# Two projection sums in the double PSUM bank, and a mean square scaled in two steps

## The chip, the core and the metric

The kernel runs on one core of a Trainium2 chip. The metric is the device time of one execution in microseconds (us). TensorE (PE, with its weight loads as PEld) multiplies matrices, VectorE (DVE), ScalarE (ACT) and GpSimd (POOL) do the rest, and SyncE (SP) issues most of the transfers. PSUM, which takes the results of TensorE, has eight banks of 128 x 512 fp32 numbers here.

## The reference

A decoder trunk of two layers on a sequence of 1024 rows with 1024 channels, batch 1, fp32:

```python
for layer in range(2):
    u = rmsnorm(h, norm_w[layer])
    h = h + (ssd_diffattn_mixer if layer == 0 else hgrn2_mixer)(u, ...)
return rmsnorm(h, final_norm_w)
```

Layer 0 projects `u` to a chunked state-space scan (16 heads of 64) and to a differential attention (8 heads of 128); the two branches' 1024 channels each are concatenated and mapped by one output projection, 2048 to 1024. Layer 1 is a gated linear recurrence with 16 heads of 128; its 2048 channels go through another output projection, 2048 to 1024. `rmsnorm(x, w)` is `x * rsqrt(mean(x*x) + 1e-6) * w`.

## The kernel before

Every product is done to fp32 accuracy out of three: both factors are split into a high and a low part (`w_hi`, `w_lo`, and likewise the data), and hi x hi, hi x lo and lo x hi are summed in one PSUM bank.

**Order of the work.** The program is written in order and then given to a planner. The planner simulates the engines with its own costs and, on each engine, takes the earliest written instruction that is ready and for whose new tile a buffer is free; the engines then run these orders as they are, each strictly in order. So products of the output projection stand in TensorE's queue between those of the last heads, wherever the planner saw TensorE free. Only the scan's stretch of TensorE has an order written by hand.

**PSUM.** `BANKS` gives the eight banks to three names: `pj`, two tiles of one bank; `s1`, two of one bank; `big`, two of two banks. `pj` takes sums of projections (L176 for the input projections, L187 for the output projection). `s1` takes transposes and small products. `big` takes, in layer 0, the scan's second step and the attention's scores: `att_core` asks for two `big` tiles for each of its eight blocks of 128 queries (L613, one for each softmax map), and VectorE frees one by adding the bias and taking maxima (L617, L621). In layer 1 `hgrn_core` uses `big` three times per head (L1054, L1090, L1096, L1142).

**The output projection** (`out_proj`, once per layer) has four quarters: two halves of the 2048 input channels (first half, second half) times two halves of the 1024 output columns (`n`). A quarter is one call of `sums`: eight sums, one for each 128 rows, taken in pairs `t = 0, 2, 4, 6`. A sum is 24 matmuls of 512 columns: two weight tiles (`kq`) times four channel blocks times three products. In the first and the last pair the order is first weight tile for both sums, then second weight tile for both. A finished sum is added by VectorE to the residual `x1`, in layer 0's first half times the scan's `rs_a` (L767), in layer 1's first half as it is (L765), in both second halves at L782. The `x1` tiles are loaded at L763 into buffers that earlier work frees. The first half needs only the scan (layer 0) or heads 0 to 7 (layer 1), so its products can run while the last heads are still computed; the data come in by `load_y` (L706 to L713). The input projections of attention head 7 are the last users of `pj` ahead of it (L579, L580 take them out).

**The norm that follows.** In the second half, ScalarE squares each updated row block and sums it (L784) into `ss[hf][:, t, n]`. When `n = 1` is done, VectorE adds the two halves (L789), scales and adds the epsilon (L149, in `rstd`), and GpSimd raises to the power -1/2 (L150). The result scales the rows: for layer 1's input (L877, L879) or for the output (L1001, L1002, stored at L1004).

Of the kernel before, what the change touches and what calls it, by code (L numbers as in the profile page):

```python
# [15 lines left out]
ALU = mybir.AluOpType  # L16
# [5 lines left out]
D = 1024  # L22
NT = L // P
KT = D // P
EPS = 1e-6
# [673 lines left out]
def load_y(S, y_d, wcols, hf, k, tags):  # L699

    nc = S.nc
    tiles = []
    for j, tag in enumerate(tags):
        y = S.t(tag, [P, 2, 512], F32R)
        raw = y[:, 1].bitcast(F32)
        nc.sync.dma_start(raw, y_d(k + j, 1)[0, :, hf * 512:hf * 512 + 512])  # L706
        if wcols is not None and k < KT:
            w = wcols[:, k + j:k + j + 1]
            nc.scalar.activation(y[:, 0], raw, AF.Identity, scale=w)
            nc.vector.scalar_tensor_tensor(y[:, 1], raw, w, y[:, 0].bitcast(F32), op0=ALU.mult, op1=ALU.subtract)  # L710
        else:
            nc.scalar.copy(y[:, 0], raw)
            nc.vector.tensor_tensor(y[:, 1], raw, y[:, 0].bitcast(F32), op=ALU.subtract)  # L713
        tiles.append(y)
    return tiles


def out_proj(S, y_d, wcols, x_d, x1_tags, rs_a, finish):


    nc = S.nc
    load = lambda hf, k, *tags: load_y(S, y_d, wcols, hf, k, tags)

    def pair():
        i = S.wpos
        S.wpos += 2
        S._wprep(i)
        S._wprep(i + 1)
        return S.wtiles[i], S.wtiles[i + 1]

    def sums(ws, ys):

        for t in range(0, NT, 2):
            pas = [S.ps("pj") for _ in range(2)]
            order = ((0, 0), (1, 0), (0, 1), (1, 1)) if t in (0, NT - 2) else ((0, 0), (0, 1), (1, 0), (1, 1))
            for j, kq in order:
                hf, tt = divmod(t + j, 4)
                y = ys[hf][4 * kq:4 * kq + 4]
                S.mm_tm(pas[j], ws[kq], *([z[:, i, tt * P:tt * P + P] for z in y] for i in range(2)),
                        first=kq == 0, last=kq == 1)  # L740
                if t == NT - 2 and j == 1:
                    S._wprep(S.wpos + kq)
                if kq == 1:
                    yield hf, tt, pas[j]

    y = [[], []]
    for hf in range(2):
        for k in range(0, KT, 2):
            y[hf] += load(hf, k, "u", "u")
        if hf == 0:  # L750
            ws = pair()

    x1s = {}
    tags = iter(x1_tags)
    late = [[], []]
    for n in range(2):
        if n:
            ws = pair()
        for hf, t, pa in sums(ws, y):
            if t % 2 == 0:  # L760
                x1 = x1s[hf, n, t // 2] = S.t(next(tags), [P, 2, 512])
                r0 = hf * 512 + t * P
                nc.sync.dma_start(x1, x_d[r0:r0 + 256, n * 512:n * 512 + 512].rearrange("(t p) n -> p t n", p=P))  # L763
            if rs_a is None:
                nc.vector.tensor_tensor(x1[:, t % 2], pa, x1[:, t % 2], op=ALU.add)  # L765
            else:
                nc.vector.scalar_tensor_tensor(x1[:, t % 2], pa, rs_a[:, hf * 4 + t:hf * 4 + t + 1], x1[:, t % 2],  # L767
                                               op0=ALU.mult, op1=ALU.add)
            if n == 1 and t % 2 == 1:
                k = 4 * hf + t - 1  # L770
                late[0] += load(0, KT + k, *(("A", "A") if k < 6 else ("u", "u")))
    tags1 = "V", "V", "G", "G", "p0", "p0", "p1", "wT"
    ss = [S.sm.tile([P, 4, 2], F32, name="ss4", bufs=2) for _ in range(2)]
    for n in range(2):
        ws = pair()
        rss = []
        for hf, t, pa in sums(ws, late):
            if n == 0 and hf == 0:
                for k in (2 * t, 2 * t + 1):
                    late[1] += load(1, KT + k, tags1[k])  # L780
            xr = x1s[hf, n, t // 2][:, t % 2]
            nc.vector.tensor_tensor(xr, pa, xr, op=ALU.add)  # L782
            jk = S.t("ey", [P, 512])
            nc.scalar.activation(jk, xr, AF.Square, accum_out=ss[hf][:, t, n:n + 1])  # L784
            if n == 0:
                finish.early(xr)
                continue
            sr = S.sm.tile([P, 1], F32, name="sr")
            nc.vector.tensor_tensor(sr, ss[hf][:, t, 0:1], ss[hf][:, t, 1:2], op=ALU.add)  # L789
            rs = S.sm.tile([P, 1], F32, name="rs")  # L790
            S.rstd(rs, sr, 1.0 / D, EPS)
            rss.append(rs)
            finish.row(hf, t, [x1s[hf, m, t // 2][:, t % 2] for m in range(2)], rs)
            if t == 3:
                finish(hf, x1s, rss)
                rss = []
# [93 lines left out]
def layer0(S, x, x1_d, u1):  # L890
# [34 lines left out]
    for h in range(8):  # L925
# [9 lines left out]
        elif h < 7:  # L935
            Vn = S.proj_v(u)
        tail = att_core(S, h, qk, V, sg[h % 2], yb[h], tail)
    tail()
    out_proj(S, lambda k, n: (ya if k < 8 else yb)[k % 8:k % 8 + n], S.ssdw, x,
             ["V", "V", "bt"] + ["A"] * 5, rsa,  # L940
             next_norm(S, u1, x1_d, S.norm_c[:, 8:16]))


def layer1(S, x1_d, u, out):
# [63 lines left out]

    finish.early, finish.row = early, row
    out_proj(S, lambda k, n: yo[k:k + n], None, x1_d, ["V", "V"] + ["A"] * 5 + ["bt"], None, finish)  # L1010


# [185 lines left out]
```

## Time and profile before

| | |
|---|---|
| median of 3 runs | 2192.46 us (2192.11 to 2192.67) |
| the profiled execution: its own time | 2190.09 us |
| its span, first to last instruction | 2188.2 us |
| TensorE busy | 2149.8 us, 98% |
| VectorE, ScalarE, GpSimd busy | 57%, 38%, 10% |
| granted TensorE clock, mean | 0.999 |

The profiled execution took 1.9 us more than its span, and 2.4 us less than the median of the runs. Times in the rows count from the span's start. A row of a timeline names the instruction's start and length, engine, line, operation, what is written `<-` what is read, and shapes; `[0.76 <-DVE w_lo L135]` says that the engine sat idle for 0.76 us before it, until that instruction ended. Lengths of matmuls overlap, since they are pipelined: back to back, one of 512 columns starts about 0.23 us after the other.

### The profile page before, as it was taken

What the parts mean: (1) busy time and instruction counts of PE and PEld (TensorE: products, weight loads), DVE (VectorE), ACT (ScalarE), POOL (GpSimd) and SP (SyncE); (2) the same over time, 40 slices, a digit from 0 to 9 for tenths busy, and PEclk for the clock granted to TensorE, in tenths of its full rate; (3) what the DMA queues carried; (4) which work ended last, traced back from release to release, by engine and by line L of the source; (5) the groups of instructions that cost most, each with busy time, mean ns of one, the idle gap of its engine ahead of it and who ended that gap; (6) DMA issues with size and microseconds to landing.
All of it is one profiled execution on the core that took longest, in us unless ns stands there. A gap on an engine that the chain in (4) does not pass through costs nothing.

```text
span 2188.2 us, 37614 instructions
## 1 busy us (share of the span) xinstructions
PE 2149.8 (98%) x15332; PEld 1827.5 (84%) x15332; DVE 1248.3 (57%) x2816; ACT 826.0 (38%) x1863; POOL 211.9 (10%) x216
## 2 busy tenths in 40 slices
PE   7999999999999999999999999999999999999998
PEld 5788888898898987877888888898989898988886
DVE  4766877565556557654344555555555555557423
ACT  4444444354445446443332233223332332234213
POOL 1021221100000000000010100101010101011000
PEclk9999999999999999999999999999999999999999
DMA  4322222322212225223221111111111111125412
GB/s 141 77 71 74 77 75 76 88 66 54 59 49 65 59 56 163 87 66 126 82 64 55 45 41 47 49 50 49 49 49 49 49 49 49 49 67 171 130 39 96
DMA packets 146752, 156.32 MB, mean 71 GB/s; under 512 B 9567, under 2 KB 113409, under 8 KB 146580
## 3 DMA queue, kind: packets, MB, share of 16 engines
q1 hardware_dynamic: 141124, 139.84, 21.4%
q0 software_dynamic: 3280, 9.90, 2.1%
q10 hardware_dynamic: 2176, 4.19, 0.5%
q8 instruction: 120, 1.97, 0.4%
q14 instruction: 52, 0.43, 0.1%
HBM read 120.08 MB, written 25.43 MB: 66 GB/s over the span
## 4 chain that ended last, share of the span: by engine, by line
PE 93%; DVE 2%; DMA 2%; ACT 2%; issue 1%; SPq 0%; POOL 0%; POOLq 0%; ACTq 0%; DVEq 0%
PE pj L176 48%; PE pj L187 26%; PE big L613 3%; PE s L649 3%; PE big L1054 2%; PE s L645 1%; PE big L1142 1%; PE big L1144 1%; PE s L1131 1%; PE big L525 1%; PE big L1096 1%; PE s L1158 1%; PE s L161 1%; PE big L519 1%; DMA A<-in_x 1%
## 5 line engine op out<-in xcount | busy, mean ns | idle before, releaser
L176 PE MATMUL pj<-u,w_hi 128*128 128x512 f32 x3072 | 980.9, 397 | 1.9 <-ACT u L163 1.2
L176 PEld LDWEIGHTS pj<-u,w_hi 128*128 128x128 f32 x3072 | 567.3, 188 | 120.8 <-issue 2.6
L176 PE MATMUL pj<-u,w_lo 128*128 128x512 f32 x1536 | 603.0, 393 | 0.0
L187 PE MATMUL pj<-w_hi,u 128*128 128x256 f32 (+1 forms) x2112 | 480.2, 316 | 2.5 <-DVE A L244 1.0
L187 PEld LDWEIGHTS pj<-w_hi,u 128*128 128x128 f32 x2112 | 350.4, 190 | 27.3 <-DVE A L244 1.4
L176 PEld LDWEIGHTS pj<-u,w_lo 128*128 128x128 f32 x1536 | 288.9, 188 | 59.9 <-issue 0.2
L187 PE MATMUL pj<-w_lo,u 128*128 128x256 f32 (+1 forms) x1056 | 331.5, 314 | 1.3 <-DVE w_lo L135 1.3
L135 DVE TENSOR_TENSOR w_lo<-w_raw,w_hi 128x1024 fp32r<-128x1024 f32 x152 | 186.0, 1244 | 136.2 <-ACT w_hi L134 136.0
L187 PEld LDWEIGHTS pj<-w_lo,u 128*128 128x128 f32 x1056 | 201.0, 190 | 13.3 <-DVE w_lo L135 2.2
L134 ACT CAST w_hi<-w_raw 128x1024 fp32r<-128x1024 f32 x152 | 152.5, 1047 | 156.8 <-PE pj L176 102.0
L243 ACT ACTIVATE th<-pj 128x512 f32<-128x512 f32 x96 | 57.2, 596 | 204.4 <-PE pj L176 204.1
L244 DVE SCALAR_TENSOR_TENSOR A<-th,pj 128x512 f32<-128x512 f32 x80 | 55.1, 688 | 136.0 <-ACT th L243 135.4
L627 ACT ACTIVATE p<-p,mx 128x256 f32<-128x256 f32 (+7 forms) x128 | 98.5, 771 | 67.8 <-DVE mx L623 60.7
L150 POOL TENSOR_TENSOR ro<-rs_t,mhalf 128x4 f32<-128x4 f32 x48 | 53.5, 1114 | 671.2 <-DVE rs_t L149 523.4
L976 POOL TENSOR_SCALAR A<-th,fN,fB 128x512 f32<-128x512 f32 x32 | 49.0, 1532 | 472.4 <-ACT th L973 464.7
L613 PE MATMUL big<-A 128*128 128x512 f32 (+3 forms) x384 | 90.0, 354 | 2.4 <-DVE mf L621 1.8
L647 ACT COPY wT<-s 128x512 f32<-128x512 f32 (+2 forms) x96 | 45.9, 478 | 96.9 <-PE s L645 96.1
L649 PE MATMUL s<-V,wT 128*128 128x128 f32 x576 | 79.6, 275 | 2.2 <-ACT wT L647 2.2
L649 PEld LDWEIGHTS s<-V,wT 128*128 128x128 f32 x576 | 75.1, 191 | 6.3 <-ACT wT L647 3.1
L1038 DVE TENSOR_TENSOR A<-A,p 128x512 f32<-128x512 f32 x96 | 65.8, 685 | 23.5 <-PE big L1054 23.0
L446 DVE SCALAR_TENSOR_TENSOR A<-V,convw,A 128x1023 f32<-128x1023 f32 (+2 forms) x48 | 61.1, 1276 | 31.7 <-ACT A L438 31.5
L1033 DVE TENSOR_TENSOR p<-p,p 128x512 f32<-128x512 f32 x96 | 66.1, 689 | 15.6 <-PE big L1090 6.5
(305 smaller groups left out, 2751.4 us busy)
## 6 DMA issues: line engine op xcount, KB each, us to landing
w_raw<-in_even_w_in SPq DMA_DIRECT2D x32, 512.0 KB, 5.4
w_raw<-in_odd_w_in SPq DMA_DIRECT2D x64, 256.0 KB, 3.6
w_raw<-in_odd_w_in SPq DMA_DIRECT2D x32, 512.0 KB, 4.2
w_raw<-in_even_w_in SPq DMA_DIRECT2D x48, 256.0 KB, 4.0
A<-A POOLq DMA_DIRECT2D x32, 256.0 KB, 5.5
w_raw<-in_even_w_out SPq DMA_DIRECT2D x16, 512.0 KB, 4.8
yo<-ey SPq DMA_DIRECT2D x32, 256.0 KB, 2.0
w_raw<-in_odd_w_out SPq DMA_DIRECT2D x16, 512.0 KB, 4.9
```

The lines of the kernel that those rows point to most:

```text
L134: nc.scalar.copy(hq, raw)
L135: nc.vector.tensor_tensor(lq, raw, hq.bitcast(F32), op=ALU.subtract)
L176: nc.tensor.matmul(out, lhsT=ww[:, k, ms], rhs=uu[k][:, sl], start=(n == 0), stop=(n == 3 * KT - 1))
L187: nc.tensor.matmul(out, lhsT=uu[k], rhs=ww[:, k, :], start=(first and k == 0 and j == 0), stop=(last and k == kt - 1 and j == 2))
L243: nc.scalar.activation(th, pj, AF.Tanh, scale=0.5)
L244: nc.vector.scalar_tensor_tensor(out, view(th), 1.0, view(pj), op0=ALU.add, op1=ALU.mult)
L446: nc.vector.scalar_tensor_tensor(cv[:, d:], rp[:, :L - d], S.convw[:, k, ci:ci + 1], cv[:, d:], op0=ALU.mult, op1=ALU.add)
L613: nc.tensor.matmul(s[:, k0:k0 + kn], lhsT=q[:, isl], rhs=ks[j][:, k0:k0 + kn], start=(j == 0), stop=(j == 1))
L627: nc.scalar.activation(p[:, :n], p[:, :n], AF.Exp, bias=mx, accum_out=z)
L649: nc.tensor.matmul(po[:, i % 4, :], lhsT=wT[:, j * P:j * P + P], rhs=V(j, hh), start=(j == 0), stop=(j == i))
L1033: nc.vector.tensor_tensor(q, q, bc(t0, [P, L // (2 * h), h]), op=ALU.mult)
L1038: nc.vector.tensor_tensor(k, k, bc(halves(Ts[h], 1)[1], [P, L // (2 * h), h]), op=ALU.mult)
```

## The change

The two sums of a quarter's first pair (`t == 0`) are put into the two banks of one `big` tile instead of two `pj` tiles; the other three pairs stay in `pj`. And in the second half, the first column half's sum of squares is multiplied by 1/1024 and given the epsilon in place by VectorE as soon as it is there; when the second half's sum comes, one operation scales it and adds the first, and GpSimd's power follows at once. `rstd` and its operation on VectorE are no longer called there.

```diff
@@ -731,7 +731,12 @@
         for t in range(0, NT, 2):
-            pas = [S.ps("pj") for _ in range(2)]
+            if t == 0:
+
+                pa = S.ps("big")
+                pas = [pa[:, 0:512], pa[:, 512:]]
+            else:
+                pas = [S.ps("pj") for _ in range(2)]
@@ -784,11 +789,14 @@
             if n == 0:
                 finish.early(xr)
+                s0 = ss[hf][:, t, 0:1]
+                nc.vector.tensor_scalar(s0, s0, 1.0 / D, EPS, op0=ALU.mult, op1=ALU.add)
                 continue
             sr = S.sm.tile([P, 1], F32, name="sr")
-            nc.vector.tensor_tensor(sr, ss[hf][:, t, 0:1], ss[hf][:, t, 1:2], op=ALU.add)
+            nc.vector.scalar_tensor_tensor(sr, ss[hf][:, t, 1:2], 1.0 / D, ss[hf][:, t, 0:1],
+                                           op0=ALU.mult, op1=ALU.add)
             rs = S.sm.tile([P, 1], F32, name="rs")
-            S.rstd(rs, sr, 1.0 / D, EPS)
+            nc.gpsimd.tensor_tensor(rs, sr, S.mhalf[:, :1], op=ALU.pow)
             rss.append(rs)
```

## Rows read from the trace of the kernel before

**Rows 1.** The page: busy time by engine, and the chain that ended last, by engine.
```profile
PE 2149.8 (98%) x15332; PEld 1827.5 (84%) x15332; DVE 1248.3 (57%) x2816; ACT 826.0 (38%) x1863; POOL 211.9 (10%) x216
...
PE 93%; DVE 2%; DMA 2%; ACT 2%; issue 1%; SPq 0%; POOL 0%; POOLq 0%; ACTq 0%; DVEq 0%
```

**Rows 2.** Stretches of layer 0: length, busy us (instructions) by engine, clock, DMA share, GB/s.
```profile
856.00:871.00 15.00, 11.48 (x64) 8.85 (x63) 13.82 (x29) 14.90 (x29) 1.03 (x2) 1.00 1.09 310
871.00:968.00 97.00, 97.00 (x507) 82.40 (x505) 51.80 (x167) 36.40 (x100) 4.17 (x5) 1.00 0.25 77
968.00:998.00 30.00, 25.22 (x141) 20.43 (x141) 25.21 (x72) 18.25 (x43) 1.62 (x2) 1.00 0.35 113
998.00:1058.00 60.00, 58.43 (x273) 47.44 (x272) 19.30 (x26) 19.56 (x44) 1.03 (x1) 1.00 0.39 123
```

**Rows 3.** Timeline, all engines, 856 to 871: start, length, instruction, idle before it.
```profile
856.25 0.39 PE L187 MATMUL pj<-w_hi,u 128*128 128x512 f32 x1
...
859.33 0.48 PE L613 MATMUL big<-A 128*128 128x256 f32 x2
...
861.93 0.50 PE L187 MATMUL pj<-w_lo,u 128*128 128x512 f32 x1 [0.76 <-DVE w_lo L135]
...
864.57 0.73 PE L187 MATMUL pj<-w_hi,u 128*128 128x512 f32 x2 [0.75 <-DVE u L710]
...
867.08 0.41 DVE L617 CUSTOM_DVE_ANT_0 p<-big,cm 128x256 f32<-128x256 f32 x1
...
867.56 0.97 PE L613 MATMUL big<-A 128*128 128x384 f32 x4 [0.46 <-DVE mx L617]
...
869.26 0.69 DVE L580 SCALAR_TENSOR_TENSOR A<-pj,A 64x512 fp32r<-64x512 f32 x1
...
870.08 1.16 PE L649 MATMUL s<-V,wT 128*128 128x128 f32 x8 [1.55 <-ACT wT L647]
...
871.10 0.48 PE L187 MATMUL pj<-w_hi,u 128*128 128x512 f32 x1
```

**Rows 4.** Timeline of VectorE, 872 to 875.
```profile
872.29 0.42 DVE L617 CUSTOM_DVE_ANT_0 p<-big,cm 128x256 f32<-128x256 f32 x1
...
872.64 0.28 DVE L621 CUSTOM_DVE_ANT_0 p<-big,far 128x128 f32<-128x128 f32 x1
...
873.88 0.75 DVE L767 SCALAR_TENSOR_TENSOR V<-pj,rsa,V 128x512 f32<-128x512 f32 x1 [0.95 <-DMA V<-in_x]
```

**Rows 5.** Timeline of TensorE, 967 to 984.
```profile
967.83 0.40 PE L187 MATMUL pj<-w_hi,u 128*128 128x512 f32 x1
...
978.89 0.65 PE L645 MATMUL s<-ident,p 128*128 128x128 f32 x4 [1.27 <-DVE p L634]
...
983.33 0.50 PE L187 MATMUL pj<-w_hi,u 128*128 128x512 f32 x1 [0.65 <-DVE A L767]
```

**Rows 6.** Stretches of layer 1, columns as in rows 2.
```profile
1998.00:2058.00 60.00, 59.54 (x522) 49.49 (x520) 40.26 (x83) 18.52 (x51) 3.63 (x3) 1.00 0.45 141
...
2093.00:2177.00 84.00, 84.00 (x370) 68.99 (x369) 29.16 (x48) 20.59 (x40) 3.28 (x6) 1.00 0.22 76
```

**Rows 7.** Chain of work that ended last: start, length, what, instructions.
```profile
2067.91 109.53 PE pj L187 x481
```

**Rows 8.** VectorE's small operations by group: busy us, mean ns, idle before.
```profile
L632 DVE SCALAR_TENSOR_TENSOR rr<-rr,z,nlam 128x1 f32<-128x1 f32 x64 | 14.0, 219 | 2.0
...
L789 DVE TENSOR_TENSOR sr<-ss 128x1 f32<-128x1 f32 x16 | 2.5, 157 | 9.5 <-ACT ey L784 9.5
...
L149 DVE TENSOR_SCALAR rs_t<-sr 128x1 f32<-128x1 f32 x16 | 2.4, 151 | 0.5
```

**Rows 9.** Timeline of VectorE at the end of the kernel.
```profile
2182.27 0.16 DVE L789 TENSOR_TENSOR sr<-ss 128x1 f32<-128x1 f32 x1 [0.85 <-ACT ey L784]
2182.46 0.15 DVE L149 TENSOR_SCALAR rs_t<-sr 128x1 f32<-128x1 f32 x1
```

**Rows 10.** Timeline of TensorE at the start of layer 1.
```profile
1108.28 0.47 PE L176 MATMUL pj<-u,w_hi 128*128 128x512 f32 x1 [0.32 <-ACT u L163]
```
## Prediction

> **What bounds the kernel now.** I read the page first. TensorE is busy for 2149.8 of 2188.2 us and makes up 93% of the chain that ended last [rows 1]: the work on TensorE sets the time, and all that a change can give is the 38 us in which it is idle, its start and end among them. A change that leaves the matmuls as they are, as this one does, can therefore win only in single idle stretches, and lose by making new ones. So next come the stretches around the output projection, by busy time of each engine [rows 2, 6]: TensorE idles 3.5 us between 856 and 871, not at all from 871 to 968, 4.8 us from 968 to 998, 1.6 us from 998 to 1058; in layer 1, 0.5 us from 1998 to 2058, and nothing from 2093 to the last sums. Last I read the timeline of the first idle stretch, with what ended each gap [rows 3].
>
> That stretch is the first pair of layer 0's first quarter. Its first sum starts at 856.25. Its second sum starts only at 871.10, because the other `pj` tile holds the last sum of head 7's projection until the operation of 869.26 has taken it out (0.69 us long, so 869.95). Meanwhile TensorE can only run ahead in the first sum: into its second weight tile, whose low part is not ready (0.76 us at 861.93), into a data tile that is not ready (0.75 us at 864.57). Then that sum is done, there is no other sum to go on with, and TensorE waits for attention's own steps, 0.46 us at 867.56 and 1.55 us at 870.08. Together 3.52 us, which is the 15.00 less 11.48 of the stretch [rows 2, 3].
>
> **The change, part by part.** *The first pair in `big`, first quarter of layer 0.* Both sums find their bank at 856, if the planner gives them a `big` tile there. A matmul of a sum costs 109.53/481 = 0.228 us [rows 7], a sum of 24 of them 5.5 us, a pair 10.9 us. The written order then holds: 24 matmuls on the first weight tile, 5.5 us of work that is ready, before the low part of the second is touched; attention's steps between, such as the scores at 859.33, push it further, to about 863 instead of 861.93, and the wait for it and for the data tile goes. The second sum's work covers the gaps of 867.56 and 870.08. Removed at most: 3.5 us; at least nothing, if ScalarE (14.90 busy of 15) and VectorE (13.82 of 15) [rows 2], which prepare the data tiles, remain late. I take 2.0 us: between the two waits of attention, which any ready matmul covers (2.0 us), and all four (3.5 us), the lower, since something of attention will be late again. From 871 to 968 TensorE is full and VectorE is busy 51.80 and ScalarE 36.40 of 97 us [rows 2], so the lead is carried on.
>
> *What it takes away there.* While the pair has a `big` tile, attention's scores have one tile in place of two. The pair keeps it from 856 until its second sum is added to `x1`. The first add waited for the transfer of `x1` until 873.88 [rows 4], so the tile comes free at about 875, after some 19 us. In that time the second, third and perhaps fourth block's scores are computed, the first of these at about 859 and the next at 867.56 [rows 3]. With one tile the second map's matmul must wait for the first map's maxima: 0.42 + 0.28 us [rows 4], and 0.46 us as TensorE waited for such maxima at 867.56 [rows 3], 1.2 us for each block, so 2.3 to 3.5 us of delay for attention; larger blocks cost more, so 4 us is the bound for a pair. It costs nothing while matmuls of sums stand in TensorE's queue; it is paid where these have run out. I take 0 and keep 4 us.
>
> *The first pairs of the other quarters.* Layer 0's second quarter starts within the 97 us in which attention goes on and TensorE is full [rows 2]: gain nothing, the same loss possible (0 to 4 us). Its last sums end at 967.83 with both `pj` tiles full, and the next matmul of a sum is at 983.33, after the add that frees one [rows 5]; the pair in `big` does not free these tiles, so 4.8 us of idle time stay. The third and fourth quarters run when attention or the recurrence has let `big` go: nothing either way. In layer 1 the first two quarters run beside heads 14 and 15, where TensorE idles 0.5 us in 60 [rows 6]; gain at most that. If `hgrn_core` waits for a tile, up to a pair's 10.9 us, the products of 110 us without a gap behind it [rows 7] take the delay. I take 0.
>
> *The mean square.* Sixteen small operations on VectorE go (the 151 ns scaling) and sixteen come (the scaling beside the products); sixteen sums of 157 ns become one operation with a factor, which no row shows in this form; bounds are 157 ns and the 219 ns of the three-operand form with a pointer [rows 8], and I take 180. At the end of the kernel the chain is sum, scaling, power, last product, store; the two starts lie 0.19 us apart [rows 9], so the chain gets 0.19 less 0.02 = 0.17 us shorter (0.13 to 0.19). At the hand-over to layer 1 TensorE waits 0.32 us for a normalised row [rows 10]; the same cut there gives 0 to 0.5 us, I take 0.2. The added scaling waits in VectorE's queue for ScalarE's sum, as the sum of now does (9.5 us over 16, 0.6 each [rows 8]), so 16 times 0.75 us; behind it stand the loads' low parts and the next add. VectorE is busy 19.30 of 60 and 29.16 of 84 us in these quarters [rows 2, 6], and half a sum more, 12 matmuls or 2.7 us, lies between one add and the next at the least, so it is hidden; without that cover it would be 6 us in each layer.
>
> *Sum.* 2.0 + 0.17 + 0.2 = 2.4 us less than the profiled execution's own 2190.09, 2187.7. Its span is 1.9 us shorter than that, and the median of the runs 2.4 us longer, so on the scale of the median the forecast is 2192.46 - 2.4 = 2190.1 us. A change of 0.2%, 4.4 us, is about what a measurement of this kernel can tell from none.
>
> **The rivals.** *The gain is given back or never made (2192.1 us).* Either the planner lets attention take the `big` tiles first, and the second pair, in `pj`, meets the same full bank until 869.95; or the lead is lost between 968 and 998, where VectorE is busy 25.21 of 30 us [rows 2] and attention's last blocks set the pace. For it: ScalarE and VectorE are nearly full from 856 to 871. Against: TensorE is full for 97 us in between. Then only 0.17 to 0.4 us of the mean square is left. [...]
>
> *Slower: attention starves for its scores' tile (2197 us).* Place: heads 6 and 7 in layer 0. Price: 4 us for each of two pairs, 8 us, less the 3.5 us won at 856 to 871, so 4.5 us on 2192.46. It shows because the sums that fill TensorE are used up at 967.83, before attention is done [rows 5]: each microsecond by which attention is later than these sums is idle time there. It decides from a delay of 2.4 us, and is beyond 4.4 us slower from some 7 us. For it: the gap of 0.46 us at 867.56 already ended with the freeing of a `big` tile [rows 3]. Against: VectorE is busy only 51.80 of 97 us there [rows 2], so maxima can be taken soon, and the delay of one pair can hide behind the pair's own matmuls.
>
> *More is won (2186 us).* Both gaps of attention's end shrink as well, because the planner, with a pair in `big`, has sums left for 968 to 998: 3.5 and about half of the 4.8 us, with 0.4 of the rest, 6.3 us. For it: a pair that attention holds back from `big` would stand ready just there. Against: its tile must be free, which attention's last blocks prevent.
>
> **How the numbers follow.** Forecast 0.44, gain lost 0.24, slower by starving 0.19, more won 0.13. The forecast's own range is 2188.3 to 2191.2 (bounds of its terms). Faster than 2188.1: all of the last case and a fifth of the forecast, 0.22. Slower than 2196.8: most of the starving case, 0.15. Within: 0.63. The range reaches up into the starving case, to 2197.5, and down to the case of more gain, to 2186.0.
>
> **What would show it.** Right: TensorE's idle time between 856 and 871 falls from 3.5 us to 1.5 or less, the second sum's matmuls start some 10 us earlier, 871 to 968 stays full, and the same instructions of layer 1 start about 2 us earlier; at the end no scaling stands between sum and power. Wrong: scores (L613) that wait for maxima with gaps of more than a microsecond, more than 4.8 us of idle time around 968 to 998, first-quarter matmuls into `big` that stand after those into `pj`, or new waits of adds behind the small scaling. The least sure part is the planner: if it orders the heads differently, gaps can come up where the change isn't.

## The result and the profile after

The changed kernel takes 2209.5 us (median of 5 runs, 2208.5 to 2211.3) against 2192.7 us (5 runs, 2192.1 to 2194.3) for the kernel before: a ratio of 1.0077, 95% interval 1.0066 to 1.0088, so 17 us slower. The forecast was 2190.1 us and its range ended at 2197.5. The profiled execution took 2209.3 us, its span is 2207.2 us.

From `sums` on, line numbers are shifted: the adds are L770 (layer 1), L772 (layer 0) and L787, ScalarE's square is L789, the sum of the two halves L796, the power L799.

**The page.** Busy time by engine, as in [rows 1]; TensorE is 93% of the chain that ended last, as before:

```profile
PE 2157.6 (98%) x15332; PEld 1834.3 (83%) x15332; DVE 1248.9 (57%) x2816; ACT 825.6 (37%) x1863; POOL 212.5 (10%) x216
```

The number of instructions on TensorE is the same, yet it is busy 7.8 us longer. So the 19.0 us by which the span grew are not idle time alone. (The medians differ by 17: the profiled execution of the kernel before, 2190.09 us, was 2.6 us faster than its median here.)

**Where.** The stretches of layer 0 and of layer 1's first quarter, columns as in [rows 2, 6], with the stretch from 871 on cut further and continued:

```profile
856.00:871.00 15.00, 12.07 (x68) 9.49 (x67) 14.37 (x34) 14.48 (x27) 1.03 (x2) 1.00 1.07 321
871.00:914.00 43.00, 43.00 (x234) 36.86 (x233) 25.09 (x89) 17.54 (x56) 3.14 (x4) 1.00 0.19 52
914.00:962.00 48.00, 31.95 (x169) 25.99 (x168) 31.73 (x118) 25.53 (x74) 2.04 (x2) 0.82 0.33 97
962.00:1000.00 38.00, 37.87 (x192) 31.67 (x191) 21.00 (x36) 15.78 (x33) 1.64 (x2) 1.00 0.41 131
...
1998.00:2058.00 60.00, 56.57 (x519) 46.72 (x518) 47.36 (x98) 24.97 (x61) 5.10 (x3) 1.00 0.47 161
```

The stretch that was full before, 871 to 968 with 97 of 97 us busy and a clock of 1.00 [rows 2], has broken: between 914 and 962 TensorE idles 16 of 48 us, and the clock granted to it is 0.82. The gap that the change aimed at, 856 to 871, is still 2.9 us (3.5 before). After 962 nearly all idle time of before is gone, but that is less than what came.

The whole of layer 0's last stage, from 856 to the first matmul of layer 1's projections (L176 at 1095.35 before, at 1112.24 after), the kernel before first:

```profile
856.00:1095.35 239.35, 229.48 (x1157) 190.02 (x1155) 125.31 (x328) 104.04 (x245) 11.21 (x16) 1.00 0.34 107
```

```profile
856.00:1112.23 256.23, 237.13 (x1165) 196.91 (x1164) 127.96 (x336) 103.30 (x245) 11.28 (x16) 0.97 0.33 102
```

It is 16.9 us longer: idle time 19.1 against 9.9 us, 9.2 more, and 7.7 us more busy time for the same work. Layer 0 thus has 16.9 of the span's 19.0 us; layer 1 has the rest. Two kernels of the experiments whose layer 0 is that of before (the mean square alone, and `big` in layer 1's first quarter alone) start layer 1's projections at 1096.63 and 1096.65, so one execution against another makes it 15.6 to 16.9 us.

Not all of the 7.7 us is the lower clock. TensorE's clock is near 0.5 in two stretches (TensorE alone: length, busy, clock, DMA share, GB/s):

```profile
920.00:930.00 10.00, 6.78 (x30) 0.51 0.26 96
940.00:947.00 7.00, 5.31 (x20) 0.51 0.29 75
```

They hold 12.1 us of busy time; if all of it would take half as long at the full clock, that is 6 us (an estimate). The rest was not separated; matmuls that stand alone overlap less with others, so that more of each one's length is counted.

**Why TensorE idles there.** TensorE from 914 on, and the first matmul of the pair in `big` (timeline: start, length, instruction, idle before it and what ended it):

```profile
914.37 0.44 PE L613 MATMUL big<-A 128*128 128x128 f32 x2
915.59 0.33 PE L613 MATMUL big<-A 128*128 128x128 f32 x1 [0.78 <-DVE mf L621]
920.36 0.44 PE L613 MATMUL big<-A 128*128 128x128 f32 x1 [4.44 <-DMA A<-A]
920.60 1.07 PE L645 MATMUL s<-ident,p 128*128 128x128 f32 x4
924.53 0.69 PE L645 MATMUL s<-ident,p 128*128 128x128 f32 x2 [2.86 <-ACT wT L647]
...
961.51 0.49 PE L187 MATMUL big<-w_hi,u 128*128 128x512 f32 x1
```

What runs between 914 and 961 is attention alone, the rest of head 6 and then head 7: scores (L613), transposes (L645, L668), values (L649), many of them waiting for data, maxima or copies. No matmul of a sum stands between them. The sums of the three pairs in `pj` ended at 909.8; the pair in `big` starts only when the last scores are done, the last of them started at 958.5 (all scores after 850: lengths in ns, first and last start):

```profile
L613 PE MATMUL big<-A x92: 220/393/775, 859.5 to 958.5; 128*128 128x512 f32 x48, 128*128 128x256 f32 x16, 128*128 128x384 f32 x16, 128*128 128x128 f32 x12
```

And the second quarter's sums, which filled this stretch before, could not start, because their weights were not ready. A weight tile is loaded in two parts into `w_raw`, then ScalarE casts them into `w_hi` and VectorE fills `w_lo`. The second quarter's first tile lies in `w_raw` early in both kernels (loads at 861.90 before, at 862.48 after); what it waits for is a free `w_hi`. ScalarE's casts of the second quarter's two tiles in the kernel before:

```profile
917.20 2.00 ACT L134 CAST w_hi<-w_raw 128x1024 fp32r<-128x1024 f32 x2 [4.59 <-PE pj L187]
925.53 1.03 ACT L134 CAST w_hi<-w_raw 128x1024 fp32r<-128x1024 f32 x1
926.76 1.05 ACT L134 CAST w_hi<-w_raw 128x1024 fp32r<-128x1024 f32 x1 [0.20 <-DMA w_raw<-in_even_w_out]
```

and in the changed kernel:

```profile
968.75 1.98 ACT L134 CAST w_hi<-w_raw 128x1024 fp32r<-128x1024 f32 x2
980.47 2.01 ACT L134 CAST w_hi<-w_raw 128x1024 fp32r<-128x1024 f32 x2 [1.04 <-PE big L187]
```

They come 52 and 54 us later, the first 7 us after the pair in `big` has started, the second when a matmul of that pair has ended. (The second tile's loads wait in turn for `w_raw`: 921.12 before, 971.78 after.) `w_hi` and `w_lo` have two buffers each, a quarter uses both (one for each `kq`), and the withheld pair is their last reader. My reading from here on, the **held weights**: attention, which is written earlier, takes every `big` tile until it is done; the withheld pair holds the quarter's weights; so six sums stand in front of attention's end and not the 14 of before, and TensorE runs out of filler. The rivals are that the lateness of a pair costs by itself, that all quarters pay alike, and that attention would idle TensorE in any case.

**The end of the kernel**, to be read beside [rows 9]:

```profile
2201.82 0.16 DVE L796 SCALAR_TENSOR_TENSOR sr<-ss 128x1 f32<-128x1 f32 x1 [0.85 <-ACT ey L789]
2202.06 0.54 POOL L799 TENSOR_TENSOR rs<-sr,mhalf 128x1 f32<-128x1 f32 x1 [2.48 <-DVE sr L796]
2202.63 0.72 ACT L1009 ACTIVATE u<-A,rs 128x512 f32<-128x512 f32 x1 [0.85 <-POOL rs L799]
```

From the start of the sum to the last products it takes 0.81 us; before, the sum began at 2182.27 [rows 9] and the products at 2183.34, 1.07 us:

```profile
2182.76 0.54 POOL L150 TENSOR_TENSOR rs<-rs_t,mhalf 128x1 f32<-128x1 f32 x1 [2.73 <-DVE rs_t L149]
2183.34 0.72 ACT L1001 ACTIVATE u<-A,rs 128x512 f32<-128x512 f32 x1 [1.10 <-POOL rs L150]
```

The second half of the change does what it says, and is worth 0.26 us there.

### The profile page after: what moved, and what is told of

Its sections match the earlier page's. It is cut to its first block, busy times and chain, and to the rows that moved or that the text cites. A ratio compares the mean times of both kernels' runs of the same rounds, so it can differ in the third digit from the quotient of the medians.

```text
span 2207.2 us, 37615 instructions
## 1 busy us (share of the span) xinstructions
PE 2157.6 (98%) x15332; PEld 1834.3 (83%) x15332; DVE 1248.9 (57%) x2816; ACT 825.6 (37%) x1863; POOL 212.5 (10%) x216
## 4 chain that ended last, share of the span: by engine, by line
PE 93%; ACT 2%; DMA 2%; DVE 2%; issue 1%; SPq 0%; POOLq 0%; POOL 0%; ACTq 0%; DVEq 0%
PE pj L176 48%; PE pj L187 24%; PE big L187 3%; PE big L613 3%; PE s L649 3%; PE big L1062 2%; PE s L645 1%; PE big L1150 1%; PE big L1152 1%; PE s L1139 1%; PE big L525 1%; PE big L1104 1%; PE s L1166 1%; DMA A<-yb 1%; DMA A<-in_x 1%
## 5 line engine op out<-in xcount | busy, mean ns | idle before, releaser
L176 PE MATMUL pj<-u,w_hi 128*128 128x512 f32 x3072 | 981.3, 397 | 2.2 <-ACT u L163 1.2
L176 PEld LDWEIGHTS pj<-u,w_hi 128*128 128x128 f32 x3072 | 567.7, 188 | 121.5 <-issue 2.6
L176 PE MATMUL pj<-u,w_lo 128*128 128x512 f32 x1536 | 603.5, 393 | 0.0
L187 PE MATMUL pj<-w_hi,u 128*128 128x256 f32 (+1 forms) x1952 | 426.2, 309 | 1.7 <-DVE A L244 1.0
L176 PEld LDWEIGHTS pj<-u,w_lo 128*128 128x128 f32 x1536 | 289.1, 188 | 60.1 <-issue 0.2
L187 PEld LDWEIGHTS pj<-w_hi,u 128*128 128x128 f32 x1952 | 320.8, 190 | 20.1 <-DVE A L244 1.4
L187 PE MATMUL pj<-w_lo,u 128*128 128x256 f32 (+1 forms) x976 | 299.7, 307 | 0.5 <-DVE w_lo L135 0.5
L187 PEld LDWEIGHTS pj<-w_lo,u 128*128 128x128 f32 x976 | 185.9, 190 | 9.8 <-DVE w_lo L135 1.4
L613 PE MATMUL big<-A 128*128 128x512 f32 (+3 forms) x384 | 91.5, 358 | 10.1 <-DMA A<-A 4.4
L649 PE MATMUL s<-V,wT 128*128 128x128 f32 x576 | 81.5, 280 | 4.0 <-ACT wT L647 4.0
L649 PEld LDWEIGHTS s<-V,wT 128*128 128x128 f32 x576 | 76.7, 196 | 8.6 <-ACT wT L647 5.5
L613 PEld LDWEIGHTS big<-A 128*128 128x128 f32 x384 | 65.3, 192 | 20.5 <-issue 6.2
```

What stands on the lines that cost most here:

```text
L176: nc.tensor.matmul(out, lhsT=ww[:, k, ms], rhs=uu[k][:, sl], start=(n == 0), stop=(n == 3 * KT - 1))
L187: nc.tensor.matmul(out, lhsT=uu[k], rhs=ww[:, k, :], start=(first and k == 0 and j == 0), stop=(last and k == kt - 1 and j == 2))
L613: nc.tensor.matmul(s[:, k0:k0 + kn], lhsT=q[:, isl], rhs=ks[j][:, k0:k0 + kn], start=(j == 0), stop=(j == 1))
L649: nc.tensor.matmul(po[:, i % 4, :], lhsT=wT[:, j * P:j * P + P], rhs=V(j, hh), start=(j == 0), stop=(j == i))
```

## The experiments

Ratios are to the kernel before on the same chip, with 95% intervals; 0.001 is 2.2 us.

### Which part, and which quarter

**The mean square alone.** `sums` as before, the other half of the change kept:

```diff
+                s0 = ss[hf][:, t, 0:1]
+                nc.vector.tensor_scalar(s0, s0, 1.0 / D, EPS, op0=ALU.mult, op1=ALU.add)
...
-            nc.vector.tensor_tensor(sr, ss[hf][:, t, 0:1], ss[hf][:, t, 1:2], op=ALU.add)
+            nc.vector.scalar_tensor_tensor(sr, ss[hf][:, t, 1:2], 1.0 / D, ss[hf][:, t, 0:1],
+                                           op0=ALU.mult, op1=ALU.add)
...
-            S.rstd(rs, sr, 1.0 / D, EPS)
+            nc.gpsimd.tensor_tensor(rs, sr, S.mhalf[:, :1], op=ALU.pow)
```

> The scaling beside the products alone, every pair of sums in two pj banks as before. Theory (the withheld pair costs everything): 0.2 to 0.3 us faster than before, since the chain from the last sr to the last product took 0.81 us in the changed kernel against 1.07 before, and TensorE's stages as before: 14 sums between 856 and 968, no idle stretch between 914 and 962. Rival (the eight added VectorE operations or the ACT chain around them cost something): slower than before by up to 2 us, in layer 1's last stage.

Measured: 2191.8 us, ratio 0.9999 (0.9989 to 1.0008). Its trace has 48.00 of 48 us busy from 914 to 962 and the same short chain at the end. The loss is not here, and 0.26 us can't be told from nothing. All further kernels have this half.

**The `big` tile in one place at a time.** The condition of the first of three kernels is shown; the second has `rs_a is None` in it, which is layer 1, the third `t == 0 and quarter > 0`, in both layers:

```diff
-            if t == 0:
+            if t == 0 and quarter == 0 and rs_a is not None:
```

> The big tile only for the first pair of layer 0's first quarter, all other pairs in pj, with the scaling. Theory (that pair waits for the end of attention, holds the quarter's two weight tiles, and so keeps the next quarter's sums from filling TensorE beside attention): the loss of the full change less layer 1's part, +13 to +15 us against before (2206 to 2208), with 6 sums in front of the stretch from 914 to 962, TensorE busy about 32 of its 48 us there and the granted clock near 0.82. Rival (all quarters pay alike, each pair waiting for its big tile): about a quarter to a half of the 17 us, +4 to +8.

> The big tile only for the first pair of layer 1's first quarter, with the scaling. Theory: the scan of the last head still holds the big tiles there, but it ends early enough: +2 to +3 us against before (the gaps of 1.48, 0.95 and some smaller ones between 2047 and 2054 in the changed kernel). Rival (the same lock as in layer 0): +8 us or more.

> The big tile in every quarter but the first of each layer, with the scaling. Theory: in layer 0 the eight sums of the first quarter and the six others of the second stand in front of the withheld pair, 14 as before, so attention's end has the same filler: within 0.5 us of before (2192.2 to 2193.2), and the second quarter's first pair simply runs after attention. Rival (any withheld pair costs): +3 us or more, in the stretch up to 968.

| `big` in | median us | ratio |
|---|---|---|
| layer 0, first quarter | 2210.8 | 1.0083 (1.0071 to 1.0096) |
| layer 1, first quarter | 2195.7 | 1.0013 (1.0004 to 1.0022) |
| second to fourth quarters of both layers | 2193.9 | 1.0006 (0.9997 to 1.0014) |

One of the eight pairs that the change moves makes the whole loss of layer 0. Its stretch from 914 to 962 is that of the full change, busy 31.83 of 48 us at a clock of 0.79; the time came out 3 us above what was expected. With `big` in all later quarters the same stretch stays filled, 46.47 of 48 us:

```profile
914.00:962.00 48.00, 46.47 (x253) 39.27 (x253) 26.26 (x87) 18.25 (x47) 2.13 (x3) 1.00 0.37 114
```

That the quarters pay alike is out. A withheld pair in the second quarter leaves 8 + 4 sums in front of attention's end (288 matmuls before the last scores, not the 14 sums that I had expected), which is nearly enough; one in the first leaves 6.

### Is it the pair's place, or what it holds?

**The last pair instead of the first**, layer 0's first quarter:

```diff
-            if t == 0:
+            if t == NT - 2 and quarter == 0 and rs_a is not None:
```

> Layer 0's first quarter alone, and there the last pair of sums in the big tile instead of the first. Theory (whichever pair is withheld holds the quarter's two weight tiles): again 6 sums in front of the stretch without filler, +15 to +18 us against before. Rival (it is the order, the first pair coming last): about before, within 1 us.

Measured: 2206.6 us, ratio 1.0060 (1.0045 to 1.0075), 13 us slower. Somewhat less than expected, but far from nothing: again 144 matmuls of sums, six sums, lie before 914, TensorE is busy 35.17 of 48 us from 914 to 962 at a clock of 0.86, and the pair starts at 959.40. So most of the loss comes without any change in which pair is first; the order of the pairs is not the cause.

**The pair as late, without the hold.** The pair in `big` is written behind the second quarter and has its two weight tiles loaded a second time for itself (two more specs of weights); the first quarter begins with `t = 2`:

```diff
+    if rs_a is not None:
+        ws = pair()
+        for hf, t, pa in sums(ws, y, 0, 2, big=True):
+            nc.vector.scalar_tensor_tensor(xa[:, t], pa, rs_a[:, t:t + 1], xa[:, t], op0=ALU.mult, op1=ALU.add)
...
-    l0 = specs + out(WO)
+    o = out(WO)
+    l0 = specs + o[:4] + o[:2] + o[4:]
```

> All of the work, with the scaling; layer 0's first pair of the first quarter in a big tile, written behind the second quarter, with its two weight tiles loaded a second time for it alone; every other pair in pj. The pair is as late as in the full change, but it holds no weights: 12 sums stand free in front of attention's end. Theory (the price is the held weights): second quarter's weights load near 915, the stretch from 914 to 962 is idle for some 4 us and not for 16, and the time is 2193 to 2197. Rival (a pair that late costs by itself, as work left over when attention ends): 2205 or more.

Measured: 2197.3 us, ratio 1.0027 (1.0014 to 1.0040), 6 us slower than before, at the upper edge of what the theory said and well below the rival's 2205. The pair is later than in the full change (its `big` matmuls start at 989.4, against 961.5), and the stretch is nearly full again, because the second quarter's weights are cast at 900.02 and 909.45:

```profile
914.00:962.00 48.00, 46.05 (x247) 39.21 (x248) 23.35 (x85) 14.20 (x42) 1.04 (x1) 1.00 0.27 84
```

```profile
900.02 1.98 ACT L134 CAST w_hi<-w_raw 128x1024 fp32r<-128x1024 f32 x2
909.45 2.00 ACT L134 CAST w_hi<-w_raw 128x1024 fp32r<-128x1024 f32 x2 [1.31 <-PE pj L187]
```

So two thirds of the loss (1.0083 to 1.0027) go when the weights are not held, though the pair is later still. What of the remaining 6 us is the second loading of weights and what the lateness was not separated.

**The hold cut short by the written order.** `out_proj` becomes a generator; its loads and its first pair are written ahead of the last head's `att_core`, everything else as in the full change:

```diff
+        if h == 7:
+            next(proj)
         tail = att_core(S, h, qk, V, sg[h % 2], yb[h], tail)
     tail()
...
+    run(proj)
```

> The full change, with layer 0's loads of y and first pair written ahead of the last head's scores and values, so that the pair's claim on a big tile comes before those of that head. Theory (what is written earlier takes the big tiles first): the pair gets its tile when the head before the last has made its scores, near 914 us instead of 961.5, the weights are free some 47 us earlier, the idle stretch nearly goes: 2193 to 2198. Rival (attention keeps the big tiles whatever the order): 2209 as in the full change.

Measured: 2192.7 us, ratio 0.9998 (0.9989 to 1.0008). Over the whole kernel the loss is gone. The pair gets its tile at 914.65, when head 6 has made its scores, 47 us earlier than in the full change:

```profile
914.65 0.51 PE L187 MATMUL big<-w_hi,u 128*128 128x512 f32 x1
```

```profile
914.00:962.00 48.00, 45.35 (x231) 38.23 (x230) 25.55 (x77) 18.29 (x46) 1.04 (x1) 0.96 0.38 110
962.00:1000.00 38.00, 36.53 (x201) 30.77 (x200) 28.91 (x77) 20.53 (x46) 1.62 (x2) 1.00 0.33 106
1000.00:1058.00 58.00, 58.00 (x269) 48.29 (x268) 19.07 (x31) 17.62 (x40) 1.03 (x1) 1.00 0.37 121
...
1998.00:2058.00 60.00, 56.15 (x501) 46.97 (x501) 40.40 (x85) 20.77 (x61) 5.26 (x5) 0.97 0.38 124
```

Here the pair holds one `big` tile while head 7 works, which is the place of my rival of the starving scores. It cost nothing that can be measured: the last scores start at 975.4, against 981.1 before.

The last of these rows shows that layer 1's loss is still there: TensorE idles 3.9 us of these 60, as in the changed kernel (3.4) and not as before (0.5). In this execution it is made up in layer 0: TensorE idles 2.7 us from 914 to 962, where it was full, but only 1.5 from there to 1058, where it idled 6.4 before [rows 2], and layer 1's projections start at 1094.14, against 1095.35 before and 1096.63 with the mean square alone. So the early pair may be worth 1 to 2 us in layer 0; with layer 1's pairs all in `pj` it was not run.

### How much filler, and what it is worth

**The pair left out.** In both kernels the 48 matmuls and the adds of layer 0's first pair are not done, so two row blocks of the output lack half of the input channels in 512 columns of layer 0's projection. One is the full change otherwise, the other has every pair in `pj`.

```diff
-        for hf, t, pa in sums(ws, y):
+        t0 = 2 if n == 0 and rs_a is not None else 0
...
+        for hf, t, pa in sums(ws, y, t0):
```

> The full change, and the first pair of layer 0's first quarter left out, matmuls and evictions both (its two tiles of the output then lack a quarter of the projection). Theory (the pair's price is that it holds the weights): the quarter's weights come free after its six sums, the second quarter's weights load at about 921 us and its sums fill TensorE, the stretch from 914 to 962 has no idle time and a clock of 1.00, so the time is that of before less 48 matmuls of 0.227 us, 2192.6 - 10.9, plus layer 1's 2 to 3 us: 2183 to 2186. Rival (attention itself runs TensorE idle there, whatever the sums do, because the big tiles are short): the loss stays and only the pair's own work goes: 2209.5 - 10.9 = 2198.6.

> The kernel with the scaling alone, every pair in pj, and the first pair of layer 0's first quarter left out (its two tiles of the output lack a quarter of the projection): 12 sums in front of the end of attention and nothing withheld. The run with the pair left out of the full change had only 10 sums there, because the second quarter's first pair was withheld in its turn, and TensorE idled again from 950 us. Theory (loss goes by how many sums stand in front: 14 none, 12 about 1 us, 6 some 17): 2193.0 - 10.9 + 1 = 2183, within 2 us. Rival (attention idles TensorE however many sums are free): 2190 or more.

Measured: 2192.8 us, ratio 0.9999 (0.9989 to 1.0009), for the first; 2189.3 us, 0.9982 (0.9973 to 0.9991), for the second. Neither number was expected by either side; both lie between, the second so near its rival's 2190 that its interval (2186.9 to 2190.8) takes it in. As differences they speak for the hold: leaving out 10.9 us of work takes 17 us off the full change (2209.5) and 21.5 us off the kernel with the one pair in `big` (2210.8). But my expectation that the time then falls to before less 10.9 us was wrong, for two reasons that the traces show. In the first kernel the second quarter's first pair is withheld in its turn: only 10 sums stand in front, the last ends at 950.4, and TensorE idles after it. In the second, 12 sums stand in front, but attention does not end earlier for it: the last scores start at 982.1, against 981.1 in the kernel before. What was left out came off in front of attention's end, and became idle time there, 3.08 us at 920.91 for one, with a clock of 0.93:

```profile
914.00:962.00 48.00, 43.89 (x219) 36.92 (x219) 22.46 (x76) 15.97 (x46) 1.94 (x3) 0.93 0.30 88
```

```profile
920.91 0.80 PE L187 MATMUL pj<-w_hi,u 128*128 128x512 f32 x1 [3.08 <-DVE A L771]
```

**Three sums for nothing.** The full change with 72 more matmuls in `pj` ahead of the first quarter's third pair (`t == 4`; the expectation calls it the last, which is `t == 6`):

```diff
+            for _ in range(dummies if t == 4 else 0):
+                pj = S.ps("pj")
+                for kq in range(2):
+                    z = ys[0][4 * kq:4 * kq + 4]
+                    S.mm_tm(pj, ws[kq], *([q[:, i, 0:P] for q in z] for i in range(2)), first=kq == 0, last=kq == 1)
+                nc.vector.tensor_copy(S.sm.tile([P, 1], F32, name="sr"), pj[:, 0:1])
...
```

> The full change and three further sums in pj (72 matmuls of layer 0's first quarter, read by one small copy each and used for nothing), written ahead of the quarter's last pair, so that 9 sums and not 6 stand in front of the stretch in which TensorE idles. Theory (idle time and the lower clock cost 9 and 8 us): the 16.3 us of dummies fit into idle time and keep the granted clock near 1.00 up to about 945, so the time does not rise by 16 us; with half of the clock's loss given back it is 2206 to 2212. Rival (the lower clock in the records costs nothing, and attention's chain sets the end): the dummies delay nothing and win nothing or they add up in full: 2209.5, or 2226.

Measured: 2214.3 us, ratio 1.0095 (1.0080 to 1.0110): 4.8 us above the full change for 72 x 0.228 = 16.4 us of matmuls. That is above my 2212 and far below 2226. TensorE's stretch from 914 to 962 is busy 41.50 us at a clock of 0.93, against 31.95 at 0.82:

```profile
914.00:962.00 48.00, 41.50 (x228) 34.54 (x228) 28.96 (x109) 22.44 (x68) 2.13 (x3) 0.93 0.28 75
```

Work worth 16.4 us is had for 4.8 (for 4 by the ratios): most of the time for it was there, idle or lost to the clock.

### What the change was to win

**The first gap closed in another way.** No `big` tile; the casts of the second half of `y` are queued on ScalarE and VectorE behind head 7's last evictions of `pj`, which are then done early:

```diff
+                S.att_last = ea.ins, ed.ins
...
+            if hf == 1 and rs_a is not None:
+                with S.tc.issue_after(S.att_last[0]), S.tc.issue_after(S.att_last[1]):
+                    y[hf] += load(hf, k, "u", "u")
```

> No big tile; the scaling, and the casts of the second half of y in layer 0's first quarter queued on ScalarE and VectorE behind the last head's last evictions of pj, so that both pj banks are free near 864 us instead of 870. This aims at the gap that the change was to close, 3.5 us between 856 and 871. Theory (the last 2.0 us of it, 0.46 and 1.55, are the full banks; the first 1.5 us are loads of weights and y): 1 to 2 us faster than the scaling alone, 2190 to 2191.5. Rival (attention takes what is won): no change, 2192 to 2193.

Measured: 2194.2 us, ratio 1.0009 (1.0001 to 1.0018), above both expectations. The gap between 856 and 871 goes from 3.52 to 0.11 us, loads included, which is more than the change was to do, and nothing is won:

```profile
856.00:871.00 15.00, 14.89 (x79) 12.24 (x78) 14.45 (x32) 14.26 (x28) 1.03 (x2) 1.00 1.10 307
871.00:914.00 43.00, 41.07 (x215) 34.87 (x214) 23.31 (x84) 15.58 (x49) 2.05 (x2) 1.00 0.14 40
914.00:962.00 48.00, 46.24 (x244) 39.08 (x243) 27.08 (x81) 19.50 (x49) 2.13 (x3) 1.00 0.38 110
```

```profile
874.99 0.50 PE L187 MATMUL pj<-w_hi,u 128*128 128x512 f32 x1 [1.93 <-DVE V L772]
```

The gap moved on: 1.93 us at 874.99, where the next pair waits for an add whose `x1` is still on its way, and 1.8 us between 914 and 962. The last scores start at 981.7, before at 981.1.

**More filler.** No `big` tile; layer 0's later loads of `y` go into `u` tiles and come behind the second quarter's second pair (the last of them behind its last pair), so that this quarter's last pair finds its `x1` tile early:

```diff
-            if n == 1 and t % 2 == 1:
+            if rs_a is not None:
+                if n == 1 and t == 3:
+                    for k in ((0, 2, 4), (6,))[hf]:
+                        late[0] += load(0, KT + k, "u", "u")
+            elif n == 1 and t % 2 == 1:
                 k = 4 * hf + t - 1
                 late[0] += load(0, KT + k, *(("A", "A") if k < 6 else ("u", "u")))
```

> No big tile; the scaling, and layer 0's loads of y for the third and fourth quarter in u tiles, written behind the second quarter's second pair, instead of in A tiles, so that the second quarter's last pair finds its x1 tile (an A) before attention ends: 16 sums in front and not 14. Theory (TensorE's idle time at the end of attention is a lack of sums): most of the 4.8 us idle between 968 and 998 goes, 2188 to 2190. Rival (those waits are attention's own chain and its last y, which more sums only push back): no change, or up to 2 us slower.

Measured: 2196.5 us, ratio 1.0016 (1.0007 to 1.0024). TensorE is full from 962 to 1000, and the idle time comes afterwards, 7.5 us from 1000 to 1058, since the last scores now start at 999.4:

```profile
962.00:1000.00 38.00, 38.00 (x198) 32.35 (x197) 24.98 (x72) 16.89 (x39) 2.04 (x2) 1.00 0.22 70
1000.00:1058.00 58.00, 50.50 (x239) 41.66 (x238) 21.49 (x47) 19.68 (x47) 1.64 (x2) 0.94 0.28 87
```

The rival was right in kind, though the loss of 3.5 us (by the ratio) is above its 2. With more sums in front attention is pushed back, and its last `y`, which the late quarters need, with it. None of these kernels beats the kernel before; the best, the scaling alone and the pair ahead of the last head, equal it.

## Why the prediction was wrong

**The step that failed.** "Both sums find their bank at 856, if the planner gives them a `big` tile there": it does not. The other branch stood among the rivals, "the planner lets attention take the `big` tiles first", and was priced at 2192.1 us because "the second pair, in `pj`, meets the same full bank", which is no loss. The price of that branch is the term that was missed, 16 to 17 us in layer 0. I asked what the pair takes from attention, and not what a pair that waits keeps from others: two weight tiles, hence eight of the 14 sums. Some 6 us of the price (the estimate above) are the lower clock, which no term of the sum held. The third rival even counted a held-back pair as a gain, as work that "would stand ready" when attention ends; it stood ready, at 961.51, and it was what had emptied the stretch before. The runs that show it are the `big` tile in layer 0's first quarter alone (all of the loss from one pair), the late pair with weights of its own (two thirds back; the last third stays open), and the pair ahead of the last head (all of layer 0's loss back).

**The lead that is carried on.** "From 871 to 968 TensorE is full ..., so the lead is carried on" was the argument for the 2.0 us. Even where the gap is closed (0.11 us left) the time does not fall. There the stage ends with attention's last scores and what follows them, and their last start stayed put (981.7, 981.1 before). It is at 999 with 16 sums and more in front, at 981 to 982 with 14, at 975 to 982 with 12, at 976 with 10, at 964 with 9, at 956 to 959 with 6. An early end of attention is no gain by itself: with 6 sums it is the earliest and the time 13 to 18 us longer, since the sums that did not run beside it are left for later. Of the kernels that do all of the work the fastest have 12 or 14. A full TensorE in a stretch does not say that TensorE sets that stretch's end when some of its work may as well run later.

**What it takes away.** The starving scores, 4 us a pair, did not come about: in the changed kernel attention has both `big` tiles until it is done and its last scores start 22.6 us earlier than before (958.5 against 981.1), and where the pair does get a tile beside a head, the kernel is as fast as before. The price of 0 that I took was right, as far as this run tells. The range reached up to 2197.5 for this case, not for the one that came.

**The range.** The forecast's own upper end, 2191.2 us, is not the bound of its terms: with the gap's least, which was put at nothing, they give 2192.3. This does not bear on the failure.

**The other quarters.** Layer 0's second to fourth: nothing expected, 1.0006 measured. Layer 1's first quarter: "I take 0", with heads that hold `big` again, and 0.0013 measured, 3 us; its first pair also runs last, at 2052.97, and the recurrence's own steps leave gaps before it, 1.48 us the longest:

```profile
2049.84 0.96 PE L1133 MATMUL s<-ident,A 128*128 128x128 f32 x7 [1.48 <-DVE A L1046]
...
2052.97 0.48 PE L187 MATMUL big<-w_hi,u 128*128 128x512 f32 x1
```

**The mean square.** 0.17 us expected at the end, 0.26 in the trace; the operation of three operands took 0.16 us, not the 0.18 assumed, and GpSimd starts 0.24 us after the sum's start, against 0.49. As a time it can't be told from none (0.9999).

Of the signs listed as "wrong" one came: first-quarter matmuls into `big` behind those into `pj`. It was the right one to name, and it had no price. No score waited for maxima for more than 0.86 us; the longest waits of scores were for a transfer (4.44 us) and for an operation of the norm on VectorE (1.37 us).

## What to carry to other kernels

When work is moved to a buffer that earlier written work also uses, ask what the moved piece holds while it waits: an operand with two buffers, kept by one waiting reader, stops everything that comes after it. Count the filler in front of a slow chain before and after (here 14 sums and 6), and charge the idle time and the lower clock that follows it. A gap on the busiest engine is worth its length only if what ends the stage moves with it.

## What the hardware showed

The mean clock is 0.994 in the changed kernel and 0.999 before, but in this stretch it fell to its lower level. The stretch in pieces of 4 us (TensorE busy, clock, DMA share, GB/s):

```profile
914.00:918.00 4.00, 1.07 (x6) 1.00 1.06 295
918.00:922.00 4.00, 1.32 (x5) 0.70 1.06 303
922.00:926.00 4.00, 1.47 (x7) 0.50 0.12 47
926.00:930.00 4.00, 4.00 (x20) 0.52 0.00 0
930.00:934.00 4.00, 3.40 (x27) 1.00 0.00 0
934.00:938.00 4.00, 2.95 (x16) 1.00 0.01 2
938.00:942.00 4.00, 1.99 (x8) 0.76 0.00 0
942.00:946.00 4.00, 3.20 (x14) 0.50 0.50 131
```

After two pieces in which TensorE was busy 1.07 and 1.32 of 4 us the granted clock is 0.50, the lower level of 1.2 GHz. It stays there through a piece in which TensorE is busy all 4.00 us, then returns to 1.00, and falls again behind the 1.99 of 938 to 942. So work behind a hole ran at half speed, and the hole cost more than its length: the longest matmul of a score took 775 ns, against 497 before. The Trainium skill ("TensorE: Matmul & The Clock Gate", section on HAM oscillation) tells of the like: a kernel that waits for loads between short bursts of matmuls begins each burst cold. This trace agrees for the first fall, which comes in the wait of 4.44 us for a transfer; in front of the second the waits are for VectorE, 1.37 and 1.03 us.

The transfer for which head 7's scores waited 4.44 us (`A<-A`) is no slower than before: the median of its two parts from issue to landing is 6.8 us in both kernels, and the transfers of 918 to 922 run at 303 GB/s here and at 293 before. Before, TensorE had sums to run in the meantime.
